# Tree attention: half of a PSUM copy moved from VectorE to ScalarE, and the transposes moved to the front of PE's iteration

## Chip, cores, metric

One core of a Trainium2 chip. The metric is the device time of one execution in microseconds (us), the median over several. In the profile, PE is TensorE (PEld its weight loads), DVE is VectorE, ACT is ScalarE, POOL is GpSimd, SP is SyncE. The profile's span runs from the first to the last instruction; in the profiled runs here it is 2.1 to 3.4 us shorter than the time of the same execution.

## The reference, cut to what matters

```python
batch, heads, seq, dim = 8, 12, 512, 64          # Q, K, V: float32
mask[i, j] = 1 where j is i or an ancestor of i in a binary heap
scores  = einsum('bhqd,bhkd->bhqk', Q, K) / sqrt(dim) + (1 - mask) * (-1e9)
weights = softmax(scores)                          # over the keys
return einsum('bhqk,bhkd->bhqd', weights, V)
```

The kernel works on pairs of heads: 8 batches of six pairs, 48 pairs. Only keys that can be ancestors are multiplied, hence its small odd tiles.

## The kernel before

Four steps make one pair i: the transposes of Q and K into PSUM (tile tp) and their copy to SBUF (qk); the scores into PSUM (st1, stx) and three exponentials on ACT (et1, etx, ete); the products with V into PSUM (o2); and their division on DVE. DVE also rearranges V for each batch ("spreading"), in slices of three to five small copies after the division in five of six iterations. The parts that matter:

```python
psumS = tile_pool(name="psumS", bufs=1, space=PSUM)   # st1, stx
psumT = tile_pool(name="psumT", bufs=2, space=PSUM)   # tp
psumO = tile_pool(name="psumO", bufs=1, space=PSUM)   # o2
...
def transposes(i):
    ...
    tp = psumT.tile([P, 2, 512], bf16)     # Q's half, K's half: 2048 bytes a partition
    ...                                    # 8 transposes of Q, 8 of K on PE
    qk = work.tile([P, 2, 512], bf16)
    nc.vector.tensor_copy(out=qk[:, :, :], in_=tp[:, :, :])
    state[i] = qk
...
with tc.manual_schedule(engines={E.PE, E.DVE, E.Activation}):
    ...
    for i in range(N):
        b, hp = pairs[i]
        if i + 1 < N:
            scores(i + 1)          # PE: st1, stx; ACT: three exponentials
        if i + 2 < N:
            transposes(i + 2)
        values(i)                  # PE: o2; DVE: reciprocal, product; store
        ...                        # DVE: copies(todo[...]), the spreading
```

In the trace of the kernel before DVE and ACT run in the order in which this text issues their instructions (DVE's 288 after its memsets, ACT's 144 exponentials).

The softmax here doesn't subtract the row's maximum and nothing guards it: scores larger than these inputs give would overflow.

Of the kernel before, what the change touches and what calls it, by code (L numbers as in the profile page):

```python
# [123 lines left out]
def kernel(  # L124
# [7 lines left out]
    nc = tc.nc  # L132
# [57 lines left out]
    def load(b):  # L190
        qs = stage.tile([P, H, T * D], bf16)
        ks = stage.tile([P, H, T * D], bf16)
        vs = stage.tile([P, H, T * D], bf16)
        if b == 0:
            plan = ((Q, 0, 2), (K, 0, 2), (V, 0, 6), (Q, 2, 6), (K, 2, 6),
                    (V, 6, H), (Q, 6, H), (K, 6, H))
        elif b < B - 1:
            plan = ((V, 0, H), (Q, 0, 6), (K, 0, 6), (Q, 6, H), (K, 6, H))
        else:
            plan = ((V, 0, H), (Q, 0, 6), (K, 0, 6), (Q, 6, 10), (K, 6, 10),  # L200
                    (Q, 10, H), (K, 10, H))
        for src, h0, h1 in plan:
            dst = qs if src is Q else ks if src is K else vs
            nc.gpsimd.dma_start(  # L204
                out=dst[:, h0:h1, :],
                in_=src[b, h0:h1].rearrange("h (p t) d -> p h (t d)", t=T),
            )
        loaded[b] = (qs, ks, vs)

    def spread(b, half):  # L210
        vs = loaded[b][2]
        v1, vx = v1s[b % NV], vxs[b % NV]
        n = H // 2
        h0, h1 = n * half, n * half + n
        v = vs[:, h0:h1, :].rearrange("p h (t d) -> p h t d", t=T)
        ops = [(vx[64:P, h0:h1, :, 0:D], v[64:P, :, :, :])]
        for par in range(2):
            slots = slice(0, 4, 3) if par else slice(1, 3)
            for a in range(2):
                ops.append((  # L220
                    vx[32 * a:32 * a + 32, h0:h1, slots, 0:D],
                    v[32:64, :, 2 * a + par, :].unsqueeze(2).to_broadcast(
                        [32, n, 2, D]
                    ),
                ))
        for r in range(T):
            ops.append((
                v1[32 * r:32 * r + 32, h0:h1, 0:D], v[0:32, :, ORD[r], :]
            ))
        return ops  # L230

    def copies(ops):
        for o, i in ops:
            nc.vector.tensor_copy(out=o, in_=i)  # L234
# [4 lines left out]
    def transposes(i):  # L239
        b, hp = pairs[i]  # L240
        if hp == 0:
            load(b)
        qs, ks, vs = loaded[b]
        tp = psumT.tile([P, 2, 512], bf16)

        for sel, src, order in ((0, qs, ident), (1, ks, permk)):
            for t in range(T):
                for hi in range(2):
                    o = tp[D * hi:D * hi + D, sel, :]
                    if sel == 0:  # L250
                        o = o[:, P * t:P * t + P]
                    else:
                        lo = 64 * ORD[t]
                        step = 256 + 64 * t - lo
                        o = o[:, lo:].rearrange(
                            "d (c x) -> d c x", x=64
                        )[:, 0:step // 64 + 1:step // 64, :]
                    nc.tensor.matmul(  # L258
                        out=o, lhsT=src[:, 2 * hp + hi, D * t:D * t + D],
                        rhs=order, start=True, stop=True, is_transpose=True,  # L260
                    )
        qk = work.tile([P, 2, 512], bf16)
        nc.vector.tensor_copy(out=qk[:, :, :], in_=tp[:, :, :])  # L263
        state[i] = qk

    def scores(i):
# [57 lines left out]
    def values(i):  # L324
        b, hp = pairs[i]
        v1, vx = v1s[b % NV], vxs[b % NV]
        et1, etx, ete = state.pop(i)
        o2 = psumO.tile([P, 2, 512], fp32)
        for hi in range(2):
            h = 2 * hp + hi  # L330
            for t in range(T):
                w = [(et1[:, hi, P * t:P * t + P], v1[:, h, 0:D + 1]),
                     (etx[:, hi, t, :], vx[:, h, t, 0:D + 1])]
                if t < 2:
                    w.append((ete[:, hi, 96 * t:96 * t + P],
                              vx[:, h, 1 - t, 0:D + 1]))
                for n, (e, v) in enumerate(w):
                    nc.tensor.matmul(  # L338
                        out=o2[:, hi, (D + 1) * t:(D + 1) * (t + 1)],
                        lhsT=e, rhs=v, start=n == 0, stop=n == len(w) - 1,  # L340
                    )
        o4 = o2[:, :, 0:T * (D + 1)].rearrange("p h (t x) -> p h t x", t=T)
        rec = opool.tile([P, 2, T, 1], fp32)
        nc.vector.reciprocal(out=rec[:, :, :, :], in_=o4[:, :, :, D:D + 1])  # L344
        of = opool.tile([P, 2, T * D], fp32)
        nc.vector.tensor_tensor(  # L346
            out=of[:, :, :].rearrange("p h (t d) -> p h t d", t=T),
            in0=o4[:, :, :, 0:D],
            in1=rec[:, :, :, :].to_broadcast([P, 2, T, D]),
            op=ALU.mult,  # L350
        )
        nc.sync.dma_start(
            out=out[b, 2 * hp:2 * hp + 2].rearrange(
                "h (p t) d -> p h (t d)", t=T
            ),
            in_=of[:, :, :],
        )

    N = len(pairs)
    E = mybir.EngineType  # L360
    with tc.manual_schedule(engines={E.PE, E.DVE, E.Activation}):
        transposes(0)
        scores(0)
        transposes(1)
        copies(spread(0, 0))
        todo = []
        for i in range(N):
            b, hp = pairs[i]
            if i + 1 < N:
                scores(i + 1)  # L370
            if i + 2 < N:
                transposes(i + 2)
            values(i)
            if hp == 0:
                todo = spread(b, 1)
            elif hp == HP - 2 and b + 1 < B:
                todo = spread(b + 1, 0)
            if hp in (0, 1, 2):
                lo, hi = ((0,) + (3, 6, 9))[hp:hp + 2]
                copies(todo[lo:hi])  # L380
            elif hp >= HP - 2 and b + 1 < B:
                copies(todo[0:4] if hp == HP - 2 else todo[4:9])
# [30 lines left out]
```

## Time and profile before

| | before |
|---|---|
| time, median (range) | 159.24 us (158.61 to 160.22) |
| span of the profiled run, its time | 158.6 us, 160.72 us |
| DVE / PE / ACT busy | 79% / 78% / 58% of the span |
| turn of a batch (hp 0 to hp 0 of the next) | 17.0 to 18.3 us |

hp is the pair's number in its batch, 0 to 5. Two from the list of waits (who waited for whom, total us, times, longest):

```profile
PE st L273 <- DVE qk L263: 8.1, 16, 1.0
...
PE tp L258 <- DMA ks<-in_K_dram: 2.9, 5, 1.1
```

The first is what the change aims at: PE stood 8.1 us in all because the copy of the transposed pair came late from DVE.

### The profile page before, as it was taken

The numbers are of one execution on the slowest core, as the hardware profiler recorded it, in microseconds if no ns is written. First come the engines' busy times: TensorE is split into PE (matmuls) and PEld (weight loads), VectorE is DVE, ScalarE is ACT, GpSimd is POOL, SyncE is SP. The second block draws the span as 40 slices with busy tenths as digits, with TensorE's granted clock in tenths as the row PEclk, the third lists the DMA queues.
The fourth block names the chain that finished last, engine by engine and source line by source line (L and its number), as shares of the span: only waits on it lengthen the run. The fifth ranks groups of instructions, "written<-read, shape, count | busy, mean of one in ns | idle before, by whom it ended". The sixth has DMA issues, their size and how long they took to land.

```text
span 158.6 us, 6339 instructions
## 1 busy us (share of the span) xinstructions
PE 123.9 (78%) x2784; PEld 82.8 (52%) x2784; DVE 125.0 (79%) x300; ACT 92.3 (58%) x145; POOL 38.2 (24%) x49
## 2 busy tenths in 40 slices
PE   0437698987889589968978789968998787968960
PEld 0213566654556357746655565745665654645640
DVE  4104889699988999799959999799969995799951
ACT  3041357665667458766674676855866668546840
POOL 7955412322242222420224222240321000000000
PEclk9999999999999999999999999999999999999995
DMA  5999999999999999999999999999999999622432
GB/s 117 145 174 197 201 195 221 235 231 227 227 232 227 238 222 223 245 228 229 225 228 239 220 223 238 225 243 221 223 244 221 231 233 237 179 81 72 133 107 94
DMA packets 50811, 32.23 MB, mean 203 GB/s; under 512 B 1504, under 2 KB 50656, under 8 KB 50784
## 3 DMA queue, kind: packets, MB, share of 16 engines
q0 software_dynamic: 37584, 18.88, 87.9%
q1 hardware_dynamic: 13200, 12.96, 28.8%
q8 instruction: 21, 0.34, 0.8%
q14 instruction: 6, 0.05, 0.1%
HBM read 38.13 MB, written 12.58 MB: 320 GB/s over the span
## 4 chain that ended last, share of the span: by engine, by line
DMA 65%; DVE 19%; PE 6%; POOL 5%; issue 3%; POOLq 0%
DMA ks<-in_K_dram 53%; DMA qs<-in_Q_dram 12%; DVE of L346 6%; DVE vx L234 6%; DVE qk L263 3%; PE o L338 3%; DVE v L234 3%; POOL vs L204 2%; DVE rec L344 2%; POOL qs L204 2%; POOL ks L204 1%; PE tp L258 1%; PE stx L273 1%; PE st L273 1%; POOLq L397 0%
## 5 line engine op out<-in xcount | busy, mean ns | idle before, releaser
L291 ACT ACTIVATE et<-st 128x1024 bf16<-128x1024 f32 x48 | 49.1, 1023 | 60.0 <-PE st L273 60.0
L263 DVE COPY qk<-tp 128x1024 bf16<-128x1024 bf16 x48 | 32.9, 685 | 20.0 <-PE tp L258 19.3
L338 PE MATMUL o<-v,et 128*128 128x65 bf16 x384 | 36.5, 195 | 10.2 <-DVE v L234 9.1
L273 PEld LDWEIGHTS <-qk 64*64 64x64 bf16 (+1 forms) x864 | 19.9, 108 | 36.9 <-issue 20.1
L312 ACT ACTIVATE etx<-stx 128x768 bf16<-128x768 f32 x48 | 38.7, 805 | 0.0
L338 PEld LDWEIGHTS <-et 128*128 128x128 bf16 x384 | 30.7, 98 | 14.5 <-DVE v L234 10.3
L338 PE MATMUL o<-vx,etx 128*128 128x65 bf16 x384 | 36.1, 194 | 0.0
L346 DVE TENSOR_TENSOR of<-o,rec 128x512 f32<-128x512 f32 x48 | 33.2, 692 | 1.7
L234 DVE COPY vx<-vs 32x768 bf16<-32x768 bf16 (+1 forms) x80 | 33.0, 412 | 1.6
L338 PEld LDWEIGHTS <-etx 128*128 128x128 bf16 x384 | 31.4, 98 | 1.2 <-issue 1.2
L338 PE MATMUL o<-vx,ete 128*128 128x65 bf16 x192 | 27.7, 195 | 0.0
L258 PE MATMUL tp<-ctile,qs 128*64 128x128 bf16 x384 | 20.9, 232 | 8.3 <-DMA qs<-in_Q_dram 8.3
L273 PE MATMUL st<-qk 64*128 64x512 bf16 x96 | 19.2, 396 | 8.5 <-DVE qk L263 8.1
L204 POOL DMA_DIRECT2D qs<-in_Q_dram x18 | 14.9, 826 | 43.8 <-DMA vs<-in_V_dram 29.9
L258 PE MATMUL tp<-ctile,ks 128*64 128x128 bf16 x384 | 19.6, 226 | 2.9 <-DMA ks<-in_K_dram 2.9
L204 POOL DMA_DIRECT2D ks<-in_K_dram x18 | 14.6, 809 | 26.4 <-DMA qs<-in_Q_dram 13.6
L273 PE MATMUL st<-ctile 64*128 64x512 bf16 x96 | 19.7, 400 | 0.3 <-issue 0.3
L273 PE MATMUL stx<-qk 64*64 64x64 bf16 (+2 forms) x768 | 19.9, 211 | 0.0
L338 PEld LDWEIGHTS <-ete 128*128 128x128 bf16 x192 | 18.4, 98 | 0.0
L234 DVE COPY v<-vs 32x384 bf16<-32x384 bf16 x64 | 17.6, 275 | 1.0
L258 PEld LDWEIGHTS <-qs 128*64 128x64 bf16 x384 | 12.8, 113 | 9.7 <-DMA qs<-in_Q_dram 8.4
L273 PE MATMUL stx<-ctile 64*128 64x448 bf16 x96 | 17.6, 363 | 0.0
(14 smaller groups left out, 59.2 us busy)
## 6 DMA issues: line engine op xcount, KB each, us to landing
out_dram<-of SPq DMA_DIRECT2D x48, 256.0 KB, 6.3
qs<-in_Q_dram POOLq DMA_DIRECT2D x14, 384.0 KB, 25.9
ks<-in_K_dram POOLq DMA_DIRECT2D x14, 384.0 KB, 26.1
vs<-in_V_dram POOLq DMA_DIRECT2D x7, 768.0 KB, 28.0
vs<-in_V_dram POOLq DMA_DIRECT2D x2, 384.0 KB, 8.9
qs<-in_Q_dram POOLq DMA_DIRECT2D x2, 256.0 KB, 17.1
ks<-in_K_dram POOLq DMA_DIRECT2D x2, 256.0 KB, 17.0
ctile<-tree_consts SPq DMA_DIRECT2D x1, 368.0 KB, 3.0
```

What stands on the lines that cost most here:

```text
L204: nc.gpsimd.dma_start(out=dst[:, h0:h1, :], in_=src[b, h0:h1].rearrange("h (p t) d -> p h (t d)", t=T),)
L234: nc.vector.tensor_copy(out=o, in_=i)
L258: nc.tensor.matmul(out=o, lhsT=src[:, 2 * hp + hi, D * t:D * t + D], rhs=order, start=True, stop=True, is_transpose=True,)
L263: nc.vector.tensor_copy(out=qk[:, :, :], in_=tp[:, :, :])
L273: nc.tensor.matmul(out=dst, lhsT=lhsT, rhs=rhs, start=first, stop=True, skip_group_check=not first,)
L291: nc.scalar.activation(out=et1[:, :, :], in_=st1[:, :, :], func=AF.Exp, scale=scale)
L312: nc.scalar.activation(out=etx[:, :, :, 32:P], in_=stx[:, :, 0:384].rearrange("p h (c q) -> p h c q", c=T), func=AF.Exp, scale=scale,)
L338: nc.tensor.matmul(out=o2[:, hi, (D + 1) * t:(D + 1) * (t + 1)], lhsT=e, rhs=v, start=n == 0, stop=n == len(w) - 1,)
L344: nc.vector.reciprocal(out=rec[:, :, :, :], in_=o4[:, :, :, D:D + 1])
L346: nc.vector.tensor_tensor(out=of[:, :, :].rearrange("p h (t d) -> p h t d", t=T), in0=o4[:, :, :, 0:D], in1=rec[:, :, :, :].to_broadcast([ ...
```

## The change

DVE is the busiest engine and the copy of tp costs it 33 us. The intent is to give half of it to ACT, which has room, and to issue a pair's transposes first in the iteration, so that the copies have a whole iteration before the scores need them.

```diff
         qk = work.tile([P, 2, 512], bf16)
-        nc.vector.tensor_copy(out=qk[:, :, :], in_=tp[:, :, :])
+        nc.vector.tensor_copy(out=qk[:, 0, :], in_=tp[:, 0, :])
+        nc.scalar.copy(out=qk[:, 1, :], in_=tp[:, 1, :])
         state[i] = qk
...
             b, hp = pairs[i]
+            if i + 2 < N:
+                transposes(i + 2)
             if i + 1 < N:
                 scores(i + 1)
-            if i + 2 < N:
-                transposes(i + 2)
             values(i)
```

## The prediction

> **What bounds the kernel now.** I read three views: the page by slices, the costliest groups, then the timeline of the last 29 us. The page first.
>
> ```profile
> PE 123.9 (78%) x2784; PEld 82.8 (52%) x2784; DVE 125.0 (79%) x300; ACT 92.3 (58%) x145; POOL 38.2 (24%) x49
> ...
> DMA  5999999999999999999999999999999999622432
> GB/s 117 145 174 197 201 195 221 235 231 227 227 232 227 238 222 223 245 228 229 225 228 239 220 223 238 225 243 221 223 244 221 231 233 237 179 81 72 133 107 94
> ```
>
> The DMA row is 9 from slice 2 to slice 34 (some 4 to 135 us) and the rate is flat at about 230 GB/s: up to 135 us the transfers are the limit, and after that the arithmetic is. The list of waits says how closely the two run together: in each batch (six pairs) PE stands for 0.2 to 1.1 us at the first pair's K transposes, for the K load. I find these at 82.56, 99.60, 116.81 and 135.04 us, 17.0, 17.2 and 18.2 us apart. So the loads allow a batch each 17.2 to 17.5 us, and the engines need hardly less: if PE's stand before the load is taken off, 17.04 us or 2.84 us a pair. **Anything that makes a pair cost more than about 2.9 us shows at once; anything that makes it cheaper meets the loads.** Now the groups and one iteration.
>
> ```profile
> L291 ACT ACTIVATE et<-st 128x1024 bf16<-128x1024 f32 x48 | 49.1, 1023 | 60.0 <-PE st L273 60.0
> L263 DVE COPY qk<-tp 128x1024 bf16<-128x1024 bf16 x48 | 32.9, 685 | 20.0 <-PE tp L258 19.3
> ...
> L312 ACT ACTIVATE etx<-stx 128x768 bf16<-128x768 f32 x48 | 38.7, 805 | 0.0
> ...
> L346 DVE TENSOR_TENSOR of<-o,rec 128x512 f32<-128x512 f32 x48 | 33.2, 692 | 1.7
> L234 DVE COPY vx<-vs 32x768 bf16<-32x768 bf16 (+1 forms) x80 | 33.0, 412 | 1.6
> ```
>
> ```profile
> 135.38 0.10 PEld L338 LDWEIGHTS <-et 128*128 128x128 bf16 x1
> ...
> 136.21 0.21 DVE L344 RECIPROCAL rec<-o 128x8 f32<-128x8 f32 x1
> ...
> 136.45 0.69 DVE L346 TENSOR_TENSOR of<-o,rec 128x512 f32<-128x512 f32 x1
> 136.55 0.35 PE L273 MATMUL stx<-ctile 64*128 64x448 bf16 x2
> 136.81 1.02 ACT L291 ACTIVATE et<-st 128x1024 bf16<-128x1024 f32 x1 [1.83 <-PE st L273]
> ...
> 137.16 0.41 PE L258 MATMUL tp<-ctile,qs 128*64 128x128 bf16 x8
> 137.17 1.64 DVE L234 COPY vx<-vs 64x1536 bf16<-64x1536 bf16 x4
> ...
> 137.73 0.81 ACT L312 ACTIVATE etx<-stx 128x768 bf16<-128x768 f32 x1
> ...
> 138.42 0.28 ACT L317 ACTIVATE ete<-stx 128x128 bf16<-128x128 f32 x1
> ...
> 138.75 0.67 DVE L263 COPY qk<-tp 128x1024 bf16<-128x1024 bf16 x1
> ```
>
> The reader is to see DVE's order: reciprocal and product of a pair, then its share of the V spreading (1.64 us here), and only then the copy of the transposed pair, which PE had finished some 0.8 us earlier. And ACT: it holds nothing but the three exponentials, 136.81 to 138.70, and waits for PE alone. **Today ACT never waits for DVE.**
>
> [...]1023 ns at 1024, 805 at 768, 284 at 128, a slope of 0.825 and 178 ns fixed.[...] the trace has one load for 144 exponentials.[...]
>
> **The change part by part.** *Removed from DVE:* half of 48 copies. 1024 elements take 685 ns; [...]512 take about 420 ns. DVE loses 48 x 0.265 = 12.7 us, from 125 to 112. *Added to ACT:* 48 copies of 178 + 0.825 x 512 = 600 ns, of which 100 ns overlap the next instruction as the exponentials do now: 24 to 29 us, from 92 to some 118. PE keeps its work. By sums alone no engine would be over 2.6 us a pair, below the loads' 2.87, and the change would seem free.
>
> *Moved, and this decides:* the order. In iteration i PE now does transposes(i+2), scores(i+1), values(i). ACT's order becomes K copy (i+2), then the exponentials of i+1. [...]the kernel's dependencies must keep the copies apart, and by program order Q's copy on DVE is first. Q's copy sits in DVE's queue behind the spreading of iteration i-1. So **the exponentials of pair i+1 now wait for the K copy, that for the Q copy, and that for reciprocal, product and spreading of pair i-1.** Pair i+1's values need these exponentials, so a loop closes from values(i-1) to values(i+1), two iterations. Its terms, from the timeline above:
> - values begin to reciprocal begins: 135.38 to 136.21 = 0.83
> - reciprocal and product: 136.21 to 137.14 = 0.93
> - spreading: six iterations of a batch have 1.65, 1.42, 1.28, 0.96, 0.78 and 0; with gaps about 0.05
> - Q copy: 0.42 + 0.03
> - K copy until the exponential may begin: 0.60 - 0.10 + 0.03 = 0.53
> - three exponentials: 136.81 to 138.70 = 1.89
> - the next pair's stx may be overwritten only now (one buffer[...]); stx begin to the end of scores is 136.55 to 137.16 = 0.61, and then values begin; hand-over 0.04.
>
> Sum without spreading: 0.83 + 0.93 + 0.05 + 0.45 + 0.53 + 1.89 + 0.65 = 5.33. A batch is six pairs, so the loop of the even pairs always meets the same spreading: 1.65 + 1.28 + 0.78 = 3.71. A batch: 3 x 5.33 + 3.71 = **19.7 us, 3.28 us a pair**; the odd pairs' loop would be 18.4, and follows the even one. That is over the loads' 17.2 to 17.5, so the loads cease to be the limit.
>
> The whole: values(0) begin at about 18.4 us as before (the first spreading ends there). From values(0) to values(46) are 23 turns: 23 x 5.33 = 122.6, and spreading 8 x 1.28 + 8 x 0.78 + 7 x 1.65 = 28.0. Values(47) follow when the one buffer of o is free, 1.76 later; then 0.83 + 0.93, and the last store's 3.44 (155.16 to 158.6): 18.4 + 150.6 + 1.76 + 1.76 + 3.44 = 176.0 us of span. The median time of before is 0.6 above its span. My terms for the two new copies and hand-overs are estimates that may each be 0.05 to 0.1 too long, 23 times over, and I shade for the rivals: **172.5 us**, 8% over 159.24.
>
> **The rivals.** *A: no coupling; the copies run side by side.* For it: the balance of engines (DVE 79%, ACT 58%), for which the change was surely made.[...] Then ACT would need some 2.45 us a pair (1.89 plus 0.6 less overlap) and the loads would still hand over K at about 135 us. Moreover PE, standing at those transposes, would have scores(41), about 1.06 us, still before it, which in the kernel before were done by then, against DVE's saving of 0.27 a pair in the last six. Little is left either way: 157.5 to 160.5. *B: the waits of PE for DVE's copy vanish.* PE waits 8.1 us in total for qk in the scores, and the new order gives the copies a whole iteration of time. True, but before 135 us the loads take it back, so at most 2 us in the last pairs: 157. It is what could make it faster if A holds. *C: ACT becomes the bound by sheer work*, 118 us of about 150: not enough by itself, only in the loop. *D: table reloads between copy and exponential*, 96 x 1.28 us: the time would be over 250; 2%.
>
> **Range and chances.** I hold the loop for about 85% sure. Within it 167 to 177. With A or B the time lies near 159, so the range of 164 to 178 leaves most of that out. Faster by over 2% needs B at its best: 0.05. Within 2%: 0.12. Slower: 0.83.
>
> **What would show it.** In the changed kernel's trace: the Q copy near 420 ns, the K copy near 600 ns; each K copy begins just after a Q copy ends; ACT's waits name DVE's copy; K-load waits on PE gone after the first batches; DMA row below 9 with a lower rate; 18.5 to 20 us a batch; DVE and ACT both near 65 to 70% of a longer span. The prediction is wrong if K copies begin before Q copies end, or if PE still stands for the K loads in each batch.

Where a cut is marked, the text rested on what no trace or run here shows. The forecast's sum came to 19.7 us a batch and 176.0 us of span, and the shading made 172.5 us of it. Cut are reasons: that for the 420 ns of the Q copy, which stand as the author's estimate (417 measured); that for the single buffer of stx; that for the order of a pair's two copies, which was an assumption (the changed kernel's trace has it in all 48 pairs); and that for expecting no further table load (that trace has one, of 1.28 us, for 48 copies and 144 exponentials). The 1023, 805 and 284 ns are ACT's three exponentials.

## More of the kernel before

Loads are issued by GpSimd, Q and K mostly in chunks of six heads and V whole; they convert float32 to bf16. By estimate some seven or eight of them are under way at a time: in the trace of the kernel before, a load lands about 26 us after its issue (median 25.9 for Q, 26.1 for K), and a batch of some 17.4 us has five.

## The result and the profile after

The changed kernel takes **182.92 us** (181.78 to 184.87, four runs, one of them slow) against 159.05 us for the kernel before in the same rounds: ratio 1.1464, 95% interval 1.1354 to 1.1573. Ratios are the mean time of one kernel's fast runs over that of the other's fast runs in the same rounds, so not quite the ratio of the medians. The direction was as predicted; the time lies outside the predicted range.

From the page of the profile after: busy time, the granted clock, DMA and rate in 40 slices, and the two new copies (count | busy us, mean ns | idle time before, releaser).

```profile
PE 131.0 (73%) x2784; PEld 92.2 (51%) x2784; DVE 111.9 (62%) x300; ACT 115.0 (64%) x193; POOL 38.7 (22%) x49
...
PEclk9999999999998899999999999969999699979996
DMA  6999999999999999999999999999933113112213
GB/s 129 148 181 197 199 217 230 227 224 226 224 227 230 219 221 226 228 224 227 226 222 233 221 226 226 224 231 216 213 98 119 60 62 120 60 62 98 81 58 117
...
L264 ACT COPY qk<-tp 128x512 bf16<-128x512 bf16 x48 | 28.4, 592 | 57.3 <-DVE qk L263 57.3
...
L263 DVE COPY qk<-tp 128x512 bf16<-128x512 bf16 x48 | 20.0, 417 | 11.6 <-PE tp L258 10.8
```

The work moved as intended: DVE fell from 125.0 to 111.9 us, ACT rose from 92.3 to 115.0. Yet no engine is above 73%. What changed is the chain of work that ended last, as the two pages give it by engine (first line before, second line after):

```profile
DMA 65%; DVE 19%; PE 6%; POOL 5%; issue 3%; POOLq 0%
DVE 27%; ACT 26%; PE 25%; issue 13%; DMA 5%; POOL 2%; ACTq 0%; POOLq 0%
```

Before, it was mostly loads; after, the three engines share it. ACT's copy of K stands 57.3 us for DVE's copy of Q. The list of waits of the changed kernel says the rest:

```profile
ACT qk L264 <- DVE qk L263: 57.3, 37, 4.9
...
DVE rec L345 <- PE o L339: 47.6, 37, 2.4
...
PE st L274 <- ACT et L292: 24.6, 22, 1.9
...
PE tp L258 <- DMA ks<-in_K_dram: 0.7, 1, 0.7
```

ACT waits for DVE, PE for ACT, and DVE for PE: a ring. PE's wait for K loads is nearly gone. One turn of the ring in the timeline (start us, us, engine, line, operation, output<-input, count, [idle before <-releaser]):

```profile
99.49 0.21 DVE L345 RECIPROCAL rec<-o 128x8 f32<-128x8 f32 x1 [1.18 <-PE o L339]
...
100.45 1.49 DVE L234 COPY vx<-vs 64x1536 bf16<-64x1536 bf16 x3
...
101.97 0.42 DVE L263 COPY qk<-tp 128x512 bf16<-128x512 bf16 x1
...
102.43 0.59 ACT L264 COPY qk<-tp 128x512 bf16<-128x512 bf16 x1 [1.70 <-DVE qk L263]
...
102.91 1.03 ACT L292 ACTIVATE et<-st 128x1024 bf16<-128x1024 f32 x1
...
104.52 0.30 ACT L318 ACTIVATE ete<-stx 128x128 bf16<-128x128 f32 x1
...
104.87 0.36 PE L274 MATMUL stx<-ctile 64*128 64x448 bf16 x2 [0.27 <-ACT ete L318]
...
106.32 0.21 DVE L345 RECIPROCAL rec<-o 128x8 f32<-128x8 f32 x1 [1.74 <-PE o L339]
```

Read it downwards: division and spreading on DVE; then Q's copy; 0.04 us after its end K's copy on ACT; then the exponentials; then stx may be overwritten; then values, and the reciprocal two pairs later. From reciprocal to reciprocal 6.83 us for two pairs (the spreading took 1.49 here; where it takes 1.28 the turn is 6.63).

### The profile page after: what moved, and what is told of

It reads as the page before. It is cut to its first block, busy times and chain, and to the rows that moved or that the text cites. A ratio compares the mean times of both kernels' runs of the same rounds, so it can differ in the third digit from the quotient of the medians.

```text
span 179.7 us, 6430 instructions
## 1 busy us (share of the span) xinstructions
PE 131.0 (73%) x2784; PEld 92.2 (51%) x2784; DVE 111.9 (62%) x300; ACT 115.0 (64%) x193; POOL 38.7 (22%) x49
## 4 chain that ended last, share of the span: by engine, by line
DVE 27%; ACT 26%; PE 25%; issue 13%; DMA 5%; POOL 2%; ACTq 0%; POOLq 0%
ACT et L292 14%; PE o L339 12%; PE stx L274 11%; DVE vx L234 11%; ACT etx L313 9%; DVE of L347 5%; DVE qk L263 5%; DMA ks<-in_K_dram 5%; DVE v L234 3%; DVE rec L345 3%; ACT ete L318 2%; PE tp L258 1%; PE st L274 1%; POOL qs L204 1%; ACT qk L264 1%
## 5 line engine op out<-in xcount | busy, mean ns | idle before, releaser
L264 ACT COPY qk<-tp 128x512 bf16<-128x512 bf16 x48 | 28.4, 592 | 57.3 <-DVE qk L263 57.3
L274 PEld LDWEIGHTS <-ctile 64*128 64x128 bf16 x192 | 15.4, 96 | 51.9 <-issue 41.7
L339 PE MATMUL o<-v,et 128*128 128x65 bf16 x384 | 38.7, 200 | 3.4 <-DVE v L234 2.1
L313 ACT ACTIVATE etx<-stx 128x768 bf16<-128x768 f32 x48 | 39.7, 828 | 0.0
L345 DVE RECIPROCAL rec<-o 128x8 f32<-128x8 f32 x48 | 9.8, 204 | 47.6 <-PE o L339 47.6
L339 PE MATMUL o<-vx,etx 128*128 128x65 bf16 x384 | 38.4, 199 | 0.0
L339 PEld LDWEIGHTS <-et 128*128 128x128 bf16 x384 | 32.3, 101 | 3.9 <-DVE v L234 1.3
L339 PEld LDWEIGHTS <-etx 128*128 128x128 bf16 x384 | 32.9, 101 | 1.3 <-issue 1.3
L339 PE MATMUL o<-vx,ete 128*128 128x65 bf16 x192 | 28.8, 200 | 0.0
L263 DVE COPY qk<-tp 128x512 bf16<-128x512 bf16 x48 | 20.0, 417 | 11.6 <-PE tp L258 10.8
L274 PE MATMUL stx<-qk 64*64 64x64 bf16 (+2 forms) x768 | 20.6, 215 | 0.0
L274 PE MATMUL st<-qk 64*128 64x512 bf16 x96 | 19.9, 404 | 0.6 <-ACT qk L264 0.6
```

Of the source, the lines that this page charges most:

```text
L263: nc.vector.tensor_copy(out=qk[:, 0, :], in_=tp[:, 0, :])
L264: nc.scalar.copy(out=qk[:, 1, :], in_=tp[:, 1, :])
L274: nc.tensor.matmul(out=dst, lhsT=lhsT, rhs=rhs, start=first, stop=True, skip_group_check=not first,)
L313: nc.scalar.activation(out=etx[:, :, :, 32:P], in_=stx[:, :, 0:384].rearrange("p h (c q) -> p h c q", c=T), func=AF.Exp, scale=scale,)
L339: nc.tensor.matmul(out=o2[:, hi, (D + 1) * t:(D + 1) * (t + 1)], lhsT=e, rhs=v, start=n == 0, stop=n == len(w) - 1,)
L345: nc.vector.reciprocal(out=rec[:, :, :, :], in_=o4[:, :, :, D:D + 1])
```

## The experiments

**Theory LOOP**: both halves of tp lie in one tile, and the two copies are ordered, DVE's first as in the text; with that, ACT's queue waits on DVE's queue, and the ring above sets the pace. In the trace of the changed kernel no K copy overlaps the Q copy of its pair, in 48 pairs. **Rivals**: the new order of PE alone (ORDER), the added 28 us of ACT work, or the clock. All kernels gave correct results.

| run | time, median us | ratio to before, 95% interval |
|---|---|---|
| changed kernel | 182.92 | 1.1464, 1.1354 to 1.1573 |
| e1_act_first | 160.12 | 1.0016, 0.9967 to 1.0065 |
| e2_two_banks | 161.41 | 1.0094, 1.0035 to 1.0154 |
| e3_order_only | 160.19 | 1.0041, 0.9994 to 1.0088 |
| e4_split_only | 163.17 | 1.0228, 1.0177 to 1.0279 |
| e5_spread_late | 161.37 | 1.0140, 1.0084 to 1.0196 |
| e6_warm | 179.24 | 1.1279, 1.1219 to 1.1339 |
| e7_act_first_hybrid | 160.88 | 1.0137, 1.0058 to 1.0216 |
| e8_hybrid_load_order | 162.38 | 1.0117, 1.0029 to 1.0205 |
| e9_hybrid_dve_copy | 159.44 | 0.9924, 0.9875 to 0.9974 |
| e10_order_hybrid | 160.46 | 1.0021, 0.9974 to 1.0068 |

The kernel before had a median of 159.55 us beside e1 to e4, 159.42 beside e5 to e8 and 160.19 beside e9 and e10.

### e1: swap the two copies

```diff
-        nc.vector.tensor_copy(out=qk[:, 0, :], in_=tp[:, 0, :])
         nc.scalar.copy(out=qk[:, 1, :], in_=tp[:, 1, :])
+        nc.vector.tensor_copy(out=qk[:, 0, :], in_=tp[:, 0, :])
```

> The changed kernel with its two copy lines swapped: ScalarE's copy of K comes first in program order, VectorE's copy of Q waits for it; [...]same work, same PE order. LOOP theory (the exponentials wait for VectorE's queue through the Q copy[...]): ACT now waits only for PE's transposes, so the 57 us of ACT qk waiting on DVE qk go to near 0, ACT needs some 2.45 us a pair, loads limit again at 17.2 to 17.6 us a batch: 158 to 162 us. Rival ORDER (the transposes in front expose PE to load waits and delay values) or ACT WORK (27 us more on ACT): stays at 178 to 185 us.

Measured: 160.12 us. Same instructions, same tile, same order on PE; only who goes first has changed, and nearly all of the loss is gone. From its list of waits:

```profile
ACT qk L263 <- PE tp L258: 29.5, 23, 4.6
...
DVE qk L264 <- ACT qk L263: 17.7, 9, 5.5
```

ACT's copy now waits for PE, and no wait of it for DVE is among the eleven largest (7.5 us and more). DVE's wait for ACT is short, because ACT reaches its copy early: of the 17.7 us, 10.2 are the two waits at the start, and the other seven are 0.3 to 2.1 us. This rules out ORDER and ACT's added work as the cause of the 24 us, since both are still in this kernel.

### e2: a tile for each half

```diff
-        tp = psumT.tile([P, 2, 512], bf16)          # psumT: bufs=2
+        tq = psumT.tile([P, 512], bf16)             # psumT: bufs=1
+        tk = psumT.tile([P, 512], bf16)
...
-        nc.vector.tensor_copy(out=qk[:, 0, :], in_=tp[:, 0, :])
-        nc.scalar.copy(out=qk[:, 1, :], in_=tp[:, 1, :])
+        nc.vector.tensor_copy(out=qk[:, 0, :], in_=tq[:, :])
+        nc.scalar.copy(out=qk[:, 1, :], in_=tk[:, :])
```

> The changed kernel with Q's and K's transposes in two tiles[...], single buffered[...], so that neither copy waits for the other. LOOP: no wait of ACT's copy for DVE's copy, 158 to 162 us. If the single buffer costs, PE shows waits at the transposes for a copy, up to 5 us more. ORDER or ACT WORK: 178 to 185 us.

Measured: 161.41 us. DVE is still first in the text, but the halves no longer share a tile, and a wait of ACT's copy for DVE's copy is not among the eleven largest (8.0 us and more); between 18 and 36 us of the trace four of five K copies begin 1.10 to 1.70 us before the Q copy of their pair. Both still write one tile qk, so that tile is not what orders them. The single buffer costs a little: PE waits 8.2 us in 13 times for the Q copy before a transpose. The longest wait of ACT's copy is now for ACT's own exponential:

```profile
ACT qk L265 <- ACT ete L319: 15.1, 25, 0.9
```

Together, e1 and e2 show that it takes both to make the ring: one shared tile tp, and DVE first. The run's name comes from the assumption that the place of the halves in PSUM orders the copies; e2 changes tile and place together, so no run shows that.

### e3 and e4: each part alone

e3 keeps the transposes in front and copies both halves on DVE again. e4 keeps the old order and splits the copy:

```diff
+        nc.vector.tensor_copy(out=qk[:, 0, :], in_=tp[:, 0, :])
+        nc.scalar.copy(out=qk[:, 1, :], in_=tp[:, 1, :])
-        nc.vector.tensor_copy(out=qk[:, :, :], in_=tp[:, :, :])
```

> Only the second part of the change: transposes in front, VectorE copies both halves as in the kernel before. LOOP: nothing couples ACT to DVE, PE's waits for qk in the scores (8 us before) vanish, loads limit; the last six pairs start one scores() later, some 1 us: 158.5 to 161.5 us. ORDER rival: most of the 24 us loss is here, 175 to 183 us.

> Only the first part: Q on VectorE, K on ScalarE[...], PE order as before (scores, transposes, values). Then ACT has the exponentials of i+1 ahead of the K copy of i+2, and the next scores wait for that copy. Estimated ring: scores to exponential 0.48, exponentials 1.89, K copy 0.55, hand-over 0.05 = 2.97 us a pair, 17.8 us a batch: 163 to 168 us, slower than before but less than the whole change. If the split alone holds the full loss: 178 to 185 us.

Measured: e3 160.19 us, not told apart from before. e4 163.17 us, 2.3% slower, with turns of 17.6 to 18.1 us a batch where 17.8 was estimated. From e4's timeline:

```profile
92.66 0.58 ACT L264 COPY qk<-tp 128x512 bf16<-128x512 bf16 x1
...
93.30 0.39 PE L274 MATMUL st<-qk 64*128 64x512 bf16 x2 [0.50 <-ACT qk L264]
93.79 1.02 ACT L292 ACTIVATE et<-st 128x1024 bf16<-128x1024 f32 x1 [0.55 <-PE st L274]
```

Here the ring is another: the K copy stands behind the exponentials in ACT's queue, PE waits for it (17.8 us in 39 times), the next exponentials wait for PE (27.2 us in 48). So the two parts cost 0.4% and 2.3% alone and 14.6% together: the order that puts K's copy in front of the exponentials is what hands DVE's lateness to them.

### e5: take the spreading out of the ring

The slices of spreading are kept back and issued after the next iteration's transposes, so that Q's copy comes before them in DVE's queue:

```diff
             if i + 2 < N:
                 transposes(i + 2)
+            copies(late)
+            late = []
...
-                copies(todo[lo:hi])
+                late = todo[lo:hi]
...                                     # the slices of hp 4 and 5 likewise
```

> The changed kernel, with each iteration's share of the V spreading moved on VectorE behind the next iteration's Q copy; the Q copy is still ahead of the K copy[...]. LOOP: the ring values, reciprocal, product, Q copy, K copy, exponentials, stx, values loses its spreading term (3.7 us a batch in the even ring) and has 5.33 us for two pairs = 16.0 us a batch, just below the loads' 17.2 to 17.6: 159 to 164 us, though ACT still waits for DVE's Q copy. If the size of the ring were set by something else (ACT's work, the clock): 175 us or more.

Measured: 161.37 us, within the expectation. ACT still waits 34.7 us for DVE's Q copy:

```profile
ACT qk L264 <- DVE qk L263: 34.7, 38, 5.3
```

But the ring without its spreading term is shorter than the loads' pace: the batches take 16.9 to 18.7 us. So a wait of that kind need cost little in itself (e5 is 1.4% slower than before, an excess that no run here divides up further); the length of the ring does.

### e6: keep PE's clock

The prediction's sum fell short. In the changed kernel the turns of the even pairs read, from DVE's timeline:

```profile
120.11 0.21 DVE L345 RECIPROCAL rec<-o 128x8 f32<-128x8 f32 x1 [1.96 <-PE o L339]
...
126.73 0.21 DVE L345 RECIPROCAL rec<-o 128x8 f32<-128x8 f32 x1 [1.38 <-PE o L339]
...
132.85 0.21 DVE L345 RECIPROCAL rec<-o 128x8 f32<-128x8 f32 x1 [2.24 <-PE o L339]
...
140.42 0.21 DVE L345 RECIPROCAL rec<-o 128x8 f32<-128x8 f32 x1 [1.88 <-PE o L339]
```

6.62, 6.12 and 7.57 us, for hp 0 to 2, 2 to 4, and 4 to the next batch's 0. The first two agree with the prediction's terms (6.61, 6.11); in other batches they reach 6.92 and 6.46. The third was to be 6.98; it is 6.87 to 7.06 in three batches and 7.48 to 7.76 in four. In those four the granted clock falls: taken by turns between 20 and 173 us, its mean is 0.72 to 0.93 in the stretches of 6 or 7 us where it falls and 1.00 in all others. Busy time by stretch for the changed kernel (the stretch and its length, busy time and instructions of PE, PEld, DVE, ACT, POOL, then the granted clock, DMA share, GB/s):

```profile
116.00:118.00 2.00, 0.73 (x6) 0.29 (x5) 1.88 (x7) 1.83 (x4) 0.00 (x0) 1.00 1.38 220
118.00:120.00 2.00, 2.00 (x38) 1.62 (x37) 0.15 (x1) 1.82 (x3) 0.00 (x0) 0.51 1.37 221
```

PE stands 1.70 us for an exponential and soon 0.27 us more, and from 118 to 121 us its clock is 0.50 to 0.52:

```profile
117.01 0.39 PE L274 MATMUL st<-ctile 64*128 64x512 bf16 x2 [1.70 <-ACT et L292]
...
117.88 0.44 PE L274 MATMUL stx<-ctile 64*128 64x448 bf16 x2 [0.27 <-ACT ete L318]
```

e6 fills those waits with dummy matmuls on constants, into a PSUM tile of their own, with tp single-buffered:

```diff
+            for _ in range({1: 4, 5: 6}.get(hp, 0)):
+                nc.tensor.matmul(out=warm[:, :], lhsT=ident, rhs=cq1,
+                                 start=True, stop=True)
```

> The changed kernel with dummy matmuls on constants[...] in PE's waits of hp 1 (four) and hp 5 (six of 0.22 us), tp single buffered[...]. They test the term that the prediction lacked: PE's waits of nearly 2 us let the granted clock fall to 0.5 for some 3 us, and the turn from hp 4 to hp 0 takes 7.5 to 7.8 us in place of 6.9 in four batches of seven. CLOCK: mean granted clock over 0.98, those turns 6.8 to 7.1 us, 178.5 to 181 us, some 2 to 4 below the changed kernel. Rival (the long turns have another cause, VectorE's spreading say): turns stay, 182 to 185 us.

Measured: 179.24 us; mean granted clock 0.999 against 0.952; the turns of hp 4 are 6.99 to 7.26. The span is 177.0 us against 179.7. The same stretches of e6:

```profile
116.00:118.00 2.00, 1.65 (x33) 0.94 (x33) 1.88 (x7) 0.85 (x2) 0.00 (x0) 1.00 1.30 243
118.00:120.00 2.00, 1.71 (x35) 1.21 (x31) 1.51 (x4) 1.91 (x3) 0.00 (x0) 1.00 1.45 199
```

So filling the waits held the clock, at 1.00 in both stretches. What that is worth can be read twice. In the changed kernel itself the four long turns average 7.62 us and the other three 6.95: four times 0.67 is 2.7 us. e6's span is 2.7 us shorter too, but 0.55 of that lies before the first reciprocal (18.43 against 18.98 us), where no dummy has run yet; its turns win 2.1, with a single buffer of tp for which PE now waits 3.7 us in 11 times. Either way the clock is real, and small beside the ring, which e6 leaves as it is. The 80 dummies added PE work and still won time.

### e7 to e10: is there a version that beats both?

With the ring gone, e1 is level with the kernel before. Its transposes stand at the batch's first K load (1.21 us, to 132.82 us of its trace) with the scores still behind them. e7 is e1 with the old order, scores first, in that one iteration of a batch. e8 is e7 with the last batch's first Q and K loads ahead of its V load.

```diff
+            first = hp == HP - 2 and b + 1 < B
+            if first:
+                scores(i + 1)
             if i + 2 < N:
                 transposes(i + 2)
-            if i + 1 < N:
+            if i + 1 < N and not first:
                 scores(i + 1)
```

> The two-line swap (K copy first) with the old PE order, scores before transposes, in the one iteration of a batch in which the transposes wait for a load. LOOP is gone as in the swap; the scores that stood behind the load wait (about 1.06 us) are taken out of the end: 158 to 160 us, up to 1 us below the swap alone. If the end is set by VectorE's order instead, no difference from the swap.

> The kernel of the run before with the last batch's first Q and K loads ahead of its V load. With the loads as the limit up to 135 us and some 20 us of pairs after the last batch's K, its first K should land some 5 us earlier and the end come 1 to 3 us sooner: 156 to 159 us. If V's later landing holds VectorE's spreading, no gain: 158 to 161 us.

Both missed: 160.88 and 162.38 us. Two of e8's four runs were slow; its fast ones took 160.24 and 161.75, not told apart from e7's. e7's reason is in its timeline (first line) and its waits (second):

```profile
134.76 0.42 DVE L264 COPY qk<-tp 128x512 bf16<-128x512 bf16 x1 [2.07 <-ACT qk L263]
DVE qk L264 <- ACT qk L263: 24.6, 9, 5.1
```

In the iteration with the old order K's copy stands behind the exponentials, Q's copy waits for K's, and the division of the pair waits behind Q's copy: the same fault with the engines exchanged. e8 still has this wait of 2.07 us, at 135.93 us of its trace; its lack of gain I did not trace further. e9 is e7 with that one pair of a batch copied whole by DVE; e10 has e7's order with all pairs copied whole by DVE.

```diff
+        if hp == 0 and b > 0:
+            nc.vector.tensor_copy(out=qk[:, :, :], in_=tp[:, :, :])
+        else:
             nc.scalar.copy(out=qk[:, 1, :], in_=tp[:, 1, :])
             nc.vector.tensor_copy(out=qk[:, 0, :], in_=tp[:, 0, :])
```

> Looks for a version that beats both. The hybrid order again, but the pair whose transposes wait for a load is copied whole by VectorE; its K copy no longer stands behind the exponentials in ACT's queue, which had VectorE waiting some 2.07 us in each batch (Q copy for K copy). REVERSED RING theory of why the hybrid gained nothing: those waits vanish, 157.5 to 160 us. If the loads alone set the end: no difference from the swap, 159.5 to 161 us.

> No copy on ScalarE at all: transposes in front except in the load-waiting iteration of a batch, VectorE copies whole. Against the run with the order alone it should win back the scores that stood behind the load, 0.5 to 1 us: 158.5 to 160 us. No coupling of ACT and DVE, so clearly below the changed kernel in any case.

Measured: e9 159.44 us, as expected, ratio 0.9924 with an interval below 1; e10 160.46, level with before, which misses its 158.5 to 160. e9's line for the same wait is

```profile
DVE qk L267 <- ACT qk L266: 11.2, 3, 6.5
```

three waits in place of nine. e9 is the best kernel, by 0.8% over the kernel before; as the best of ten tries it may owe part of that to chance. That is far less than DVE's saved time, since the loads set the pace up to about 135 us.

## Why the prediction was wrong

The mechanism held. What failed is the step from the ring to the total: the sum came to 176.0 us of span, but 4.1 us were shaded off it, 1.5 were missing from span to time, and a fall of PE's clock worth 2.7 was not in the terms. By its own steps:

- **The ring: right.** The coupling of the two copies, the wait of ACT for DVE, the vanished waits for K loads and the copies' lengths (420 and 600 ns forecast, 417 and 592 measured; with 685 ns for the whole tile, half of it costs DVE more than half) came as written. e1 and e2 show the cause, e5 the spreading term.
- **The sum of the ring: right, for a PE at full clock.** Forecast 19.7 us a batch; e6, whose clock holds, has 19.74 to 20.18, and 19.74 in its last two batches. The changed kernel has 19.9 to 20.6.
- **The missing term: PE's clock.** The steps took PE's durations from a kernel in which PE, after its start, stood at most 1.2 us at a time. The ring makes it stand up to 1.9 us, and in four turns of seven (from hp 4 to the next hp 0) its clock falls to half (0.50 from 57 to 60 us, 0.50 to 0.52 from 118 to 121, 0.51 from 138.5 to 142, 0.50 from 159 to 162.4). By those four turns this is 2.7 us of span; e6 shows the cause.
- **The shading: wrong, and the largest part.** The sum gave 176.0 us of span. I wrote 172.5 as the time, because the new terms "may each be 0.05 to 0.1 too long" and for the rivals' sake. No row supported that, and the rivals are other outcomes, to be put into chances, not into the middle. It took off 4.1 us (176.6 to 172.5), and the upper end of 178 left no room above the sum either.
- **Span to time: wrong by 1.5 us.** I set the span of one run (158.6) against the median of others (159.24) and called 0.6 the difference. The profiled run itself took 160.72, so 2.1.

Added up from the profiled run: 172.5 + 4.1 of shading + 1.5 of span to time + 2.7 of clock = 180.8; that run took 181.78. The last 1.0 is in the other turns: the 23 turns take 154.4 us in place of 150.6, which is 2.7 of clock and 1.1 of first batches and stretched spreading (1.49 us above in place of 1.28), while the first pair came 0.25 us sooner than forecast. The median of all runs is 1.1 above that run.

One reading was too strong: PE does not stand for the K load "in each batch" of the kernel before. Its trace has five such waits, at 13.21, 30.08, 82.56, 116.82 and 135.04 us; at 99.60 there is none. (The transposes of its shown iteration end 0.95 us before their copy, not 0.8.) And some signs that I gave were wrong. Most turns of a batch are above the 18.5 to 20 us, and DVE and ACT end at 62 and 64%, just below 65. The DMA row did not fall below 9 while the engines were the limit: it stays 9 at some 225 GB/s for 28 slices, to about 130 us. By the estimate above seven or eight loads are under way at a time, which may be why the row stayed full; no run isolates it. The loads even end sooner than in the kernel before, where it was about 135 us; a slower pace of stores is a likely reason, which no run here isolates. The sign that told the truth was PE's wait for K loads, 2.9 us before and 0.7 after. The rate, some 225 GB/s against 230, would have misled as the row did.

Rival A of the prediction (no coupling: 157.5 to 160.5 us) describes e1 and e2 within 1 us: without the ring the loads set the pace and the saved DVE time is worth nothing that these runs can tell from noise.

## What to carry to other kernels

When a piece of work moves to another engine, ask not only what it costs there but what its first instruction waits for: here the K copies in ACT's queue waited 57.3 us in all for DVE, and the exponentials behind them waited too. If two engines take turns at one tile, let the one that reaches its turn first go first, or give each a tile; swapping two lines was worth 22.8 us here, two tiles 21.5. When a ring has been summed up from measured rows, keep the sum, and widen the range upwards for what the ring's waits may do to PE's clock: here it fell to half in four turns, worth 2.7 us.

## Three measurements to keep

- The clock: in the changed kernel PE stood 1.70 us, worked 0.6 us, stood 0.27 us, and the clock was at 0.5 within 1 us of that. Such a fall came in four batches of seven; filling the waits with dummy matmuls (e6) held the mean at 0.999. How short the waits or how long the work between them must be to prevent the fall, no run here shows.
- The order of the two readers of one tile: 57.3 us of ACT's waiting and 14.6% of the time here, against 0.2% with the other reader first.
- The difference between span and device time: 2.1 to 2.4 us in most runs but 3.4 in one of e7's and 3.7 in one of the kernel before. It hides gains of that size in a span alone: in the profiled runs e7's span is 1.9 us below that of the kernel before, its time only 0.6.
